# Softmax sums on VectorE, a 16-row tile inside v's projection, weight splits in quarters: one change to a hybrid decoder block

## The chip, the cores and the metric

The kernel runs on one core of one Trainium2 chip. The metric is the device time of one execution in microseconds (us). TensorE is written PE, its weight loads PEld, VectorE DVE, ScalarE ACT, GpSimd POOL, SyncE SP.

## The reference

One decoder block on 1,024 tokens of width 1,024, all in float32, with 16 meta tokens put in front (1,040 rows):

```python
h = rmsnorm(x, norm_g)
proj = jnp.einsum('bld,dn->bln', h, w_in)
u_pool, z_pool, q, k, v, z_attn, f_logit, g_pool, g_attn = jnp.split(proj, _split_points(), axis=-1)
y_pool = causal_multiscale_pool(u_pool, pool_w, pool_scale) * jax.nn.silu(z_pool)
log_f = jax.nn.log_sigmoid((f_logit + b_forget).astype(jnp.float32))
y_attn = forgetting_attention(q, k, v, log_f).reshape(B, L, ATTN_WIDTH) * jax.nn.silu(z_attn)
merged = (jax.nn.sigmoid(g_pool) * jnp.einsum('blc,cd->bld', y_pool, w_up_pool)
          + jax.nn.sigmoid(g_attn) * jnp.einsum('blc,cd->bld', y_attn, w_up_attn))
return x + jnp.einsum('bld,de->ble', merged, w_out)
```

The attention has 8 heads of width 64. Its logits get the running sum of `log_f`, a causal mask and a softmax over the keys. A last rmsnorm follows.

## The kernel before

Every float32 product is made of three products of float32r operands: each operand is split into a high part (a copy rounded to float32r) and a low part (the operand less its high part), and PE adds high x high, high x low and low x high (`g_mm3`, L131, the matmul in L139). So each weight matrix costs one copy on ACT (L127, tile `whi`) and one subtraction on POOL (L128, tile `wlo`, 128x1024 elements in one operation).

**Prologue.** Nine tiles of x (eight of 128 rows, the last of 16) are loaded, normalised (`norm_stat`, `norm_scale`) and turned by PE against an identity matrix (`norm_t`, L187, into the PSUM tiles `pt` and `pn`). ACT copies the result as `hh` (L189), DVE subtracts for `hl` (L190). Between these tiles stand the projections of q, k and v for the first pair of heads, in four column pieces each (the list `todo`; n counts them). In this part the order on all engines is the one in which the code stands (`manual_schedule`). `norm_t` of the last tile, with 16 rows, comes after piece n = 8 (v, columns 512 to 767), and piece n = 9 (q, columns 768 to 1039) needs its `hh`. Behind the last piece the weights of the forget gate are loaded (`wf`) and split by DVE (`wfs`, L443 and L444), and PE multiplies with them (L456, function `gates`).

**Attention.** From here on only PE's order is the code's; a scheduler sets the order on DVE, ACT, POOL and SP. There are 16 units: 4 pairs of heads x 2 heads x 2 halves of 512 queries, with 5 or 9 blocks of 128 keys. The steps of unit i + 1 that make logits (`qk`: PE L540 and L541 into `ps`, ACT L549 or DVE L547 into `S`, the maximum over blocks `m` on DVE, L556) are interleaved with the steps of unit i that make the softmax (`soft`: DVE L580 subtracts the maximum, ACT L581 takes the exponential, ACT L584 and DVE L585 split it into `ph` and `pl`, POOL L593 adds it up over the blocks in `acc`, PE L601 multiplies with v into `po`). Between the steps PE is given matmuls of projections that are not yet needed (`Fill`, `F.pull`), whose weights come through L127 and L128. They take most of PE's time.

At the end of a unit `maxes` (L561 to L571) takes the maximum over the 128 keys of `m`: DVE transposes 32x32 blocks into `mt`, reduces them (`mr`), combines the four groups of partitions with small copies and maxima (`mx`, `ms`, `my`, `mz`) and transposes back into the PSUM tile `pt`, from which the next unit's `soft` subtracts. `finish` evacuates `po` and sums `acc` over its 128 partitions:

```python
nc.scalar.copy(up_[:nu], acc[64:])
nc.vector.tensor_tensor(acc[:nu], acc[:nu], up_[:nu], op=ALU.add)
nc.scalar.activation(fold[:64], acc[:64], AF.Copy)
nc.vector.tensor_tensor(fold[64:], acc[:64], r32(fold)[:64], op=ALU.subtract)
```

(L614 to L617; the tiles are named `pl` and `ph` after the buffers that they share). One matmul with ones (`total`, L621, into `pt`) then sums the partitions, and ACT (L623, `ls`) and a DMA bring one row of 512 sums to DRAM (`sums`).

**End.** After the last unit come the rest of the projections, the pooling mixer (DVE L757, POOL L722), the reciprocal of the sums (L830, `lall`, stored as `recs`), the gates, the up projections (`up`, with `up_weights`) and the output projection (L892) with the final norm. `recs` is read back as `rc`, broadcast over 64 partitions (L739).

Of the kernel before, what the change touches and what calls it, by code (L numbers as in the profile page):

```python
# [8 lines left out]
F32 = mybir.dt.float32  # L9
# [10 lines left out]
H = 8  # L20
# [17 lines left out]
NPH = 3  # L38
LAG = 2
NRC = 2  # L40
REC0 = 2
EVAC = (((0, 1),), ((0,), (1,)))
WARM = (4, 1)

# [1 line left out]
def r32(ap):  # L46
    return ap.bitcast(F32)
# [7 lines left out]
def tile_hybrid_block(ctx, tc, x, meta, norm_g, w_in, b_forget, pool_w, pool_scale,  # L55
# [60 lines left out]
    hh = [hh4[k // 4][:, k % 4, :] for k in range(KO)]  # L116
    hl = [hl4[k // 4][:, k % 4, :] for k in range(KO)]

    def split_w(srcs, pool=None, tags=("wh", "wl"), eng=None):
# [7 lines left out]
        nc.scalar.activation(hi, raw, AF.Copy)  # L127
        (eng or nc.gpsimd).tensor_tensor(lo, raw, r32(hi), op=ALU.subtract)  # L128
        return hi, lo

    def w_chunk(col, **kw):  # L131
# [16 lines left out]
    def run(g):  # L148
        for _ in g:
            pass  # L150
# [28 lines left out]
    def norm_t(i0, xt, n):  # L179
        c0 = i0 * 128  # L180
        for j in range(2):
            if (2 * i0 + j) % 3 == 2:
                pt = psG.tile([128, 4, 128], F32, name="pn")
            else:
                pt = psT.tile([128, 4, 128], F32, name="pt")
            for i in range(4):
                nc.tensor.transpose(pt[:, i, :n], xt[:n, (4 * j + i) * 128:(4 * j + i + 1) * 128], ident[:n, :n])  # L187
            h_ = hh4[j][:, :, c0:c0 + n]
            nc.scalar.activation(h_, pt[:, :, :n], AF.Copy)  # L189
            last = nc.vector.tensor_tensor(hl4[j][:, :, c0:c0 + n], pt[:, :, :n], r32(h_), op=ALU.subtract)  # L190
        return last
# [200 lines left out]
    def ntok(i):  # L392
        return min(128, L - 128 * i)
# [41 lines left out]
    G_.close()  # L435
# [4 lines left out]
    wf = sm.tile([128, KO, H], F32, name="wf", bufs=1)  # L440
    nc.sync.dma_start(wf, w_in2[:, :, COL_F:COL_F + H])
    wfs = sm.tile([128, KO, 2 * H], F32R, name="wfs", bufs=1)
    nc.vector.tensor_copy(wfs[:, :, :H], wf)  # L443
    nc.vector.tensor_tensor(wfs[:, :, H:], wf, r32(wfs[:, :, :H]), op=ALU.subtract)  # L444
    SM.close()

    def gates():
# [15 lines left out]
        z, lf, u, d, one, car = [sm.tile([KB, NB, H], F32, name=n, bufs=1) for n in ("fz", "lf", "fu", "fd", "fo", "car")]  # L463
# [33 lines left out]
    pwl = sm.tile([128, 4, 128], F32R, name="pwl", bufs=1)  # L497

    exps, dves = [], []
    sums = dr.tile([H, SEQ], F32, name="sums")  # L500
    recs = dr.tile([H, SEQ], F32, name="recs")
    for p in range(4):
        spill["y", p] = dr.tile([128, SEQ], F32, name=f"sp_y{p}")

    class Unit:
# [98 lines left out]
        def finish(self):  # L604
            hr, lr = rows(self.e)
            po, acc = self.po, self.acc
            t = ap_.tile([128, 512], F32, name="t")
            nc.scalar.activation(t[hr], po[lr], AF.Copy)
            nc.vector.tensor_tensor(t[hr], po[hr], t[hr], op=ALU.add)
            nc.sync.dma_start(spill["y", self.p][hr, self.q0:self.q0 + 512], t[hr])  # L610
            fold = ap_.tile([128, 512], F32R, name="ph", bufs=NPH)
            up_ = r32(ap_.tile([128, 512], F32R, name="pl", bufs=NPH))
            nu = KB - 64
            nc.scalar.copy(up_[:nu], acc[64:])  # L614
            nc.vector.tensor_tensor(acc[:nu], acc[:nu], up_[:nu], op=ALU.add)  # L615
            nc.scalar.activation(fold[:64], acc[:64], AF.Copy)
            nc.vector.tensor_tensor(fold[64:], acc[:64], r32(fold)[:64], op=ALU.subtract)  # L617

            def total():
                pr = psT.tile([128, 512], F32, name="pt")  # L620
                nc.tensor.matmul(pr, onesr, fold, start=True, stop=True)  # L621
# [5 lines left out]
            return [total]  # L627

    def merged(a, c, extra=()):
        extra = list(extra)  # L630
# [7 lines left out]
        for i, (_, (w, dve, pe, f)) in enumerate(sorted(out_, key=lambda t: t[0])):  # L638
            f()
            if i >= REC0 and extra:  # L640
                extra.pop(0)()
            F.pull(max(0.0, PACE * dve - pe))

    cols = {"gp": COL_GP, "ga": COL_GA, "za": COL_ZA, "zp": COL_Z}
# [21 lines left out]
    late = []  # L666
    for i, u in enumerate(units):
        nxt = units[i + 1] if i + 1 < 16 else None
        F.now = i
        if nxt is not None and nxt.p != u.p:  # L670
            F.until(f"q{nxt.p}", f"k{nxt.p}")
        merged(list(nxt.a_steps()) if nxt else [], list(u.c_steps()), late)
# [8 lines left out]
        late = u.finish()  # L681
        if nxt is not None and nxt.p != u.p:
            F.until(f"v{nxt.p}")
            pair_fill(nxt.p + 1)
    for f in late:
        f()
    F.drain()
    last_dve = dves[-1]
    A.close()
# [45 lines left out]
    def attn_out(p):  # L735
        rc = btile("rc")
        for e in range(2):
            h = 2 * p + e
            after(nc.sync.dma_start(rc[rows(e)[0]], recs[h:h + 1, :].to_broadcast([64, SEQ])), stores[-1])  # L739
# [85 lines left out]
    split2 = pool_split(2)  # L825
    silu(zp[3])
    silu(zp[2])
    lall = sm.tile([128, 64], F32, name="lall", bufs=1)
    nc.sync.dma_start(lall, sums.rearrange("h (a b) -> (h a) b", b=64))
    after(nc.vector.reciprocal(lall, lall), split2)  # L830
# [127 lines left out]
```

## Time and profile before

| | |
|---|---|
| median of 3 runs | 767.85 us (767.46, 769.21, 767.85) |
| the profiled execution | 769.11 us, of which the span from the first to the last instruction is 767.4 us |
| mean granted PE clock in it | 0.997 of full speed |
| busy share of the span | PE 98%, PEld 83%, DVE 65%, ACT 51%, POOL 36% |

A line of a timeline gives start and duration in us, the engine, the line of the code, the operation, `out<-in`, the shapes and the number of instructions merged; in square brackets stands the idle time of the engine before it and who ended it. A line of the groups gives the busy time in us and the mean of one in ns, then the idle time before them. A line of the chain gives start, duration, engine, tile, line and count. PE's matmuls are pipelined, so the duration of one is longer than the step from one start to the next; how fast PE works is read from the steps.

### The profile page before, as it was taken

To read this page: it belongs to the slowest core of one execution; us is meant where nothing else is said; L and a number is where in the kernel's file an instruction comes from. 1 tells how busy PE (TensorE), PEld (TensorE's weight loads), DVE (VectorE), ACT (ScalarE), POOL (GpSimd) and SP (SyncE) were. 2 spreads that over 40 slices of the span, in tenths; PEclk is the share of its full clock that TensorE was granted. 3 is DMA by queue.
4 is the path that set the end of the run, shared out by engine and by line. 5 is a ranking of instruction groups with operands and counts; after the bars stand their busy time and mean duration, and the time that the engine had idled before them with its cause. 6 is when DMAs were issued, how large, how long until landed. Compare 5 with 4: busy or idle time off the path is not lost.

```text
span 767.4 us, 10526 instructions
## 1 busy us (share of the span) xinstructions
PE 751.6 (98%) x3762; PEld 638.5 (83%) x3762; DVE 497.1 (65%) x933; ACT 394.6 (51%) x756; POOL 278.1 (36%) x227
## 2 busy tenths in 40 slices
PE   8999999999999999999999999999999999999996
PEld 6996989988888898888988888888888688888885
DVE  5653578659779888598688866882465566434232
ACT  6652556456566655665655556551744554323112
POOL 4321235346326435433354263342374122322111
PEclk9999999999999999999999999999999999999999
DMA  9301122231221222221223232339357654523331
GB/s 304 73 18 39 28 82 74 67 97 49 62 58 52 72 75 70 77 63 41 77 62 103 71 103 62 103 108 373 123 176 177 233 176 128 191 83 113 107 110 55
DMA packets 73782, 79.33 MB, mean 103 GB/s; under 512 B 5473, under 2 KB 56673, under 8 KB 73730
## 3 DMA queue, kind: packets, MB, share of 16 engines
q1 hardware_dynamic: 68976, 63.46, 27.0%
q10 hardware_dynamic: 4754, 15.21, 6.0%
q8 instruction: 29, 0.48, 0.3%
q14 instruction: 23, 0.19, 0.1%
HBM read 57.58 MB, written 21.07 MB: 102 GB/s over the span
## 4 chain that ended last, share of the span: by engine, by line
PE 79%; DVE 8%; ACT 2%; issue 2%; DMA 2%; POOL 1%; POOLq 0%; DVEq 0%; SPq 0%; ACTq 0%
PE pj L139 57%; PE pj L892 12%; PE po L601 4%; PE ps L541 2%; PE ps L540 2%; DVE pl L585 1%; DVE S L580 1%; DMA rl<-sp_gp 1%; PE pj L456 1%; DVE ka L243 1%; POOL yl L722 1%; ACT S L549 1%; DMA rc<-recs 1%; DVE m L556 1%; DVE acc L615 0%
## 5 line engine op out<-in xcount | busy, mean ns | idle before, releaser
L139 PE MATMUL pj<-hh,whi 128*128 128x512 f32 (+4 forms) x768 | 179.9, 362 | 1.7 <-ACT hh L189 1.1
L139 PE MATMUL pj<-hl,whi 128*128 128x512 f32 (+4 forms) x768 | 178.0, 361 | 0.0
L139 PE MATMUL pj<-hh,wlo 128*128 128x512 f32 (+4 forms) x768 | 175.7, 360 | 0.0
L128 POOL TENSOR_TENSOR wlo<-raw,whi 128x1024 fp32r<-128x1024 f32 x37 | 91.7, 2478 | 223.7 <-ACT whi L127 90.5
L139 PEld LDWEIGHTS pj<-hh,whi 128*128 128x128 f32 x768 | 132.8, 190 | 19.6 <-ACT hh L189 1.2
L139 PEld LDWEIGHTS pj<-hh,wlo 128*128 128x128 f32 x768 | 133.2, 190 | 18.2
L139 PEld LDWEIGHTS pj<-hl,whi 128*128 128x128 f32 x768 | 132.5, 190 | 17.7
L585 DVE TENSOR_TENSOR pl<-S,ph 128x512 fp32r<-128x512 f32 (+4 forms) x112 | 87.1, 793 | 19.9 <-ACT ph L584 18.9
L593 POOL TENSOR_TENSOR acc<-acc,S 128x272 f32<-128x272 f32 (+4 forms) x80 | 77.5, 969 | 12.6 <-ACT S L581 6.6
L549 ACT ACTIVATE S<-ps,negc 128x400 f32<-128x400 f32 (+2 forms) x96 | 49.1, 515 | 46.7 <-DVE S L547 40.4
L581 ACT ACTIVATE S<-S 128x512 f32<-128x512 f32 (+4 forms) x112 | 49.4, 477 | 29.0 <-DVE S L580 28.9
L556 DVE TENSOR_TENSOR m<-m,S 128x272 f32<-128x272 f32 (+4 forms) x80 | 46.7, 583 | 22.3 <-ACT S L549 21.0
L584 ACT ACTIVATE ph<-S 128x512 fp32r<-128x512 f32 (+4 forms) x112 | 52.4, 478 | 11.6 <-PE po L601 10.8
L580 DVE TENSOR_TENSOR S<-S,pt 128x512 f32<-128x512 f32 (+4 forms) x112 | 51.7, 498 | 0.8
L892 PE MATMUL pj<-woh,gl 128*128 128x512 f32 (+1 forms) x136 | 51.8, 381 | 0.0
L892 PE MATMUL pj<-wol,gh 128*128 128x512 f32 (+1 forms) x136 | 51.6, 379 | 0.0
L892 PE MATMUL pj<-woh,gh 128*128 128x512 f32 (+1 forms) x136 | 51.6, 379 | 0.0
L816 POOL TENSOR_TENSOR gl<-rl,gh 128x512 fp32r<-128x512 f32 x16 | 23.2, 1454 | 72.3 <-ACT gh L815 72.3
L294 ACT ACTIVATE st<-pj 128x512 f32<-128x512 f32 x48 | 28.4, 592 | 39.7 <-PE pj L139 21.5
L127 ACT ACTIVATE whi<-raw 128x1024 fp32r<-128x1024 f32 x37 | 39.0, 1054 | 17.2 <-PE pj L139 10.6
L812 DVE TENSOR_TENSOR rl<-pj,rl 128x512 f32<-128x512 f32 x32 | 22.0, 689 | 31.8 <-PE pj L139 28.4
L540 PE MATMUL ps<-qa,ka 128*128 128x512 f32 (+4 forms) x112 | 36.4, 325 | 2.2 <-ACT S L549 2.1
(168 smaller groups left out, 1136.4 us busy)
## 6 DMA issues: line engine op xcount, KB each, us to landing
raw<-in_w_in_dram SPq DMA_DIRECT2D x40, 512.0 KB, 4.0
sp_gp<-st SPq DMA_DIRECT2D x16, 256.0 KB, 2.0
sp_ga<-st SPq DMA_DIRECT2D x16, 256.0 KB, 4.5
rl<-sp_gp ACTq DMA_DIRECT2D x8, 512.0 KB, 3.8
rl<-sp_ga ACTq DMA_DIRECT2D x8, 512.0 KB, 4.6
rawo<-in_w_out_dram SPq DMA_DIRECT2D x8, 512.0 KB, 3.1
xr<-in_x_dram SPq DMA_DIRECT2D x8, 512.0 KB, 4.3
xt<-in_x_dram SPq DMA_DIRECT2D x7, 512.0 KB, 8.3
```

Of the source, the lines that this page charges most:

```text
L127: nc.scalar.activation(hi, raw, AF.Copy)
L128: (eng or nc.gpsimd).tensor_tensor(lo, raw, r32(hi), op=ALU.subtract)
L139: nc.tensor.matmul(ps, a, b, start=(i == 0), stop=(i == len(seq) - 1))
L540: nc.tensor.matmul(ps[:kb, c0:], ka[:, k0:k0 + kb], qa[:, q0 + c0:q0 + 512], start=True, stop=False)
L549: nc.scalar.activation(s[:kb, f0:], ps[:kb, f0:], AF.Identity, bias=nb_)
L556: nc.vector.tensor_tensor(m[:kb, c0:], m[:kb, c0:], s[:kb, c0:], op=ALU.max)
L580: nc.vector.tensor_tensor(s[:kb, c0:], s[:kb, c0:], self.pm[:kb, c0:], op=ALU.subtract)
L581: exps.append(nc.scalar.activation(s[:kb, c0:], s[:kb, c0:], AF.Exp))
L584: nc.scalar.activation(ph[:kb, c0:], s[:kb, c0:], AF.Copy)
L585: dves.append(nc.vector.tensor_tensor(pl[:kb, c0:], s[:kb, c0:], r32(ph[:kb, c0:]), op=ALU.subtract))
L593: nc.gpsimd.tensor_tensor(acc[:kb, c0:], acc[:kb, c0:], s[:kb, c0:], op=ALU.add)
L892: nc.tensor.matmul(ps[:, :c1 - c0], mg[k][a][:, r], wo[k][b][:, c0:c1], start=(k == 0 and n == 0), stop=(k == KO - 1 and n == 2))
```

## The change

1. **Sums.** `finish` no longer folds `acc` and PE no longer sums it. DVE transposes `acc` in 32x32 blocks into a tile of the name `mt` and reduces it to 128x16 (`sr`); a DMA stores these partial sums, 64 bytes for each partition. `total`, `late`, the argument `extra` of `merged` and the constant `REC0` go. Before the reciprocal, four DMAs (one for each pair of heads) load the partial sums as 128x256 (`fin`), DVE adds the groups of four, takes the reciprocal and transposes 128x64 back.
2. **16-row tile.** `norm_t` of the last tile is called in the middle of piece n = 8, behind 16 of its 24 matmuls, in place of behind it.
3. **Gate weights.** The load of `wf` stands in piece n = 4, the split `wfs` in piece n = 8.
4. **Weight splits.** L128 becomes four operations of 128x256. The splits of the first three matrices (L383) stay whole.
5. Five small tiles of `gates` become slices of one tile `fz`, whose place `fin` takes later.

The words that came with the change also name four pool up projections ahead. The code of `up`, of `up_weights` and of the loop that calls them is the same in both files, and on PE no matmul behind the last unit stands in another place.

```diff
         nc.scalar.activation(hi, raw, AF.Copy)
-        (eng or nc.gpsimd).tensor_tensor(lo, raw, r32(hi), op=ALU.subtract)
+        for k in range(0, KO, 2):
+            nc.gpsimd.tensor_tensor(lo[:, k:k + 2], raw[:, k:k + 2], r32(hi[:, k:k + 2]), op=ALU.subtract)
...
-            run(v_piece(0, wv, t0, t1))
-        i = {0: 2, 1: 3, 3: 4, 4: 5, 6: 6, 7: 7, 8: 8}.get(n)
+            g = v_piece(0, wv, t0, t1)
+            if n == 8:
+                for _ in range(2 * KO):
+                    next(g)
+                norm_t(8, xts[8], ntok(8))
+            run(g)
+        i = {0: 2, 1: 3, 3: 4, 4: 5, 6: 6, 7: 7}.get(n)
...
+        if n == 4:
+            wf = sm.tile([128, KO, H], F32, name="wf", bufs=1)
+            nc.sync.dma_start(wf, w_in2[:, :, COL_F:COL_F + H])
+        if n == 8:
+            wfs = sm.tile([128, KO, 2 * H], F32R, name="wfs", bufs=1)
+            nc.vector.tensor_copy(wfs[:, :, :H], wf)
+            nc.vector.tensor_tensor(wfs[:, :, H:], wf, r32(wfs[:, :, :H]), op=ALU.subtract)
...
-            nc.scalar.copy(up_[:nu], acc[64:])
-            nc.vector.tensor_tensor(acc[:nu], acc[:nu], up_[:nu], op=ALU.add)
-            nc.scalar.activation(fold[:64], acc[:64], AF.Copy)
-            nc.vector.tensor_tensor(fold[64:], acc[:64], r32(fold)[:64], op=ALU.subtract)
...
-                nc.tensor.matmul(pr, onesr, fold, start=True, stop=True)
-                ls = ap_.tile([1, 512], F32, name="ls")
-                nc.scalar.copy(ls, pr[:1])
-                h = 2 * self.p + self.e
-                nc.sync.dma_start(sums[h:h + 1, self.q0:self.q0 + 512], ls)
+            at = ap_.tile([KB, 512], F32, name="mt")
+            after(nc.vector.transpose(at, acc), dves[-1])
+            r = sm.tile([128, 16], F32, name="sr")
+            nc.vector.tensor_reduce(r, at.rearrange("p (j b) -> p j b", b=32), axis=AX.X, op=ALU.add)
+            nc.sync.dma_start(sums[4 * self.p + 2 * self.e + self.half], r)
...
-    nc.sync.dma_start(lall, sums.rearrange("h (a b) -> (h a) b", b=64))
-    after(nc.vector.reciprocal(lall, lall), split2)
-    nc.sync.dma_start(recs.rearrange("h (a b) -> (h a) b", b=64), lall)
+    for p in range(4):
+        nc.sync.dma_start(lall[32 * p:32 * p + 32],
+                          sums[4 * p:4 * p + 4].rearrange("u (a r) j -> r u a j", r=32))
+    after(nc.vector.tensor_reduce(rall.rearrange("p (u j) -> p u j", u=4), lall.rearrange("p u a j -> p u j a"),
+                                  axis=AX.X, op=ALU.add), split2)
+    nc.vector.reciprocal(rall, rall)
+    nc.vector.transpose(fin[:, 320:], rall)
+    nc.sync.dma_start(recs.rearrange("(b p) r -> p b r", p=128), rect)
```

What this does to the order of instructions is shown at three places. The first is PE in the prologue, at the end of piece n = 8 (the rows of `pj` with 256 columns) and the start of piece n = 9 (272 columns); a row `x4` is four matmuls, and `-` and `+` are before and the change:

```order
+L187 MATMUL pt<-ident,xt 128x16 x4
+L187 MATMUL pn<-ident,xt 128x16 x4
 L139 MATMUL pj<-hh_112,wlo 128x256 x4
 L139 MATMUL pj<-hh_113,wlo 128x256 x4
-L187 MATMUL pt<-ident,xt 128x16 x4
-L187 MATMUL pn<-ident,xt 128x16 x4
 L139 MATMUL pj<-hh_112,whi 128x272 x4
 L139 MATMUL pj<-hh_113,whi 128x272 x4
```

The eight transposes of the 16-row tile move ahead of the last eight matmuls of the v piece, so that these stand between the transposes and the q piece that needs `hh`.

The second is DVE at the end of the prologue. Before:

```order
L190 TENSOR_TENSOR hl_114<-pt,hh_112 128x4x16
L190 TENSOR_TENSOR hl_115<-pn,hh_113 128x4x16
L222 SCALAR_TENSOR_TENSOR ql<-pj,qa 64x272 x2
L243 TENSOR_TENSOR ka<-pj,ka 64x272 x2
L262 TENSOR_TENSOR V<-pj,V 128x2x64 x2
L443 CAST wfs<-wf 128x8x8
L444 TENSOR_TENSOR wfs<-wf,wfs 128x8x8
```

The same place with the change:

```order
L190 TENSOR_TENSOR hl_114<-pt,hh_112 128x4x16
L190 TENSOR_TENSOR hl_115<-pn,hh_113 128x4x16
L443 CAST wfs<-wf 128x8x8
L444 TENSOR_TENSOR wfs<-wf,wfs 128x8x8
L222 SCALAR_TENSOR_TENSOR ql<-pj,qa 64x272 x2
L243 TENSOR_TENSOR ka<-pj,ka 64x272 x2
L262 TENSOR_TENSOR V<-pj,V 128x2x64 x2
```

The two operations on the gate weights pass the six operations that belong to the last q, k and v pieces.

The third is DVE between the first unit and the second, where the maximum of the next unit is finished. Before:

```order
L556 TENSOR_TENSOR m<-m,S 128x16
L615 TENSOR_TENSOR acc<-acc,pl 64x512
L561 STREAM_TRANSPOSE mt<-m 128x512
L563 TENSOR_REDUCE mr<-mt 128x16
L617 TENSOR_TENSOR ph<-acc,ph 64x512
L565 COPY mx<-mr 64x16 x2
L566 TENSOR_TENSOR ms<-mr,mx 128x16
L568 COPY my<-ms 32x16 x4
L569 TENSOR_TENSOR mz<-ms,my 128x16
L571 STREAM_TRANSPOSE pt<-mz 128x512
```

The same place with the change:

```order
L565 TENSOR_TENSOR m<-m,S 128x16
L570 STREAM_TRANSPOSE mt<-m 128x512
L572 TENSOR_REDUCE mr<-mt 128x16
L574 COPY mx<-mr 64x16 x2
L621 STREAM_TRANSPOSE mt<-acc 128x512
L575 TENSOR_TENSOR ms<-mr,mx 128x16
L623 TENSOR_REDUCE sr<-mt 128x16
L577 COPY my<-ms 32x16 x4
L578 TENSOR_TENSOR mz<-ms,my 128x16
L580 STREAM_TRANSPOSE pt<-mz 128x512
```

Two operations on `acc` stood ahead of `pt` before, two other ones stand there now, and both now come behind `mx`; the scheduler does the same at nearly all unit ends. On PE the one thing that changes behind the prologue is that the 16 matmuls with ones are gone.

More of the change, by code (lines that the diff above doesn't have):

```diff
@@ L40 @@
 NRC = 2
-REC0 = 2
 EVAC = (((0, 1),), ((0,), (1,)))
@@ L439, in tile_hybrid_block @@
     nc.sync.dma_start(psc, pool_scale[0].rearrange("(g c) -> c g", c=128))
[L440 to L444, printed above, removed]
     SM.close()
@@ L462, in gates @@
             nc.tensor.transpose(pt[:, b * 16:(b + 1) * 16], fT[:, KS[b]:KS[b] + KB], ident[:16, :16])
-        z, lf, u, d, one, car = [sm.tile([KB, NB, H], F32, name=n, bufs=1) for n in ("fz", "lf", "fu", "fd", "fo", "car")]
+        fz = sm.tile([KB, 384], F32, name="fz", bufs=1)
+        z, lf, u, d, one = [fz[:, n * NB * H:(n + 1) * NB * H].rearrange("p (b h) -> p b h", h=H) for n in range(5)]
+        car = sm.tile([KB, NB, H], F32, name="car", bufs=1)
         pv = pt[:, :NB * 16].rearrange("p (b j h) -> p b j h", j=2, h=H)
@@ L499, in tile_hybrid_block @@
     exps, dves = [], []
-    sums = dr.tile([H, SEQ], F32, name="sums")
-    recs = dr.tile([H, SEQ], F32, name="recs")
+    sums = dr.tile([16, 128, 16], F32, name="sums")
+    recs = dr.tile([256, 32], F32, name="recs")
     for p in range(4):
@@ L610, in finish, with merged @@
             nc.sync.dma_start(spill["y", self.p][hr, self.q0:self.q0 + 512], t[hr])
[L611 to L615, printed above, removed]
-            nc.scalar.activation(fold[:64], acc[:64], AF.Copy)
[L617 to L621, printed above, removed]
-                ls = ap_.tile([1, 512], F32, name="ls")
-                nc.scalar.copy(ls, pr[:1])
-                h = 2 * self.p + self.e
-                nc.sync.dma_start(sums[h:h + 1, self.q0:self.q0 + 512], ls)
-            return [total]
-    def merged(a, c, extra=()):
-        extra = list(extra)
+            at = ap_.tile([KB, 512], F32, name="mt")
[3 more added lines that the diff above has]
+            nc.sync.dma_start(sums[4 * self.p + 2 * self.e + self.half], r)
+    def merged(a, c):
         out_ = []
@@ L637, in merged @@
                 acc += s[0]
-        for i, (_, (w, dve, pe, f)) in enumerate(sorted(out_, key=lambda t: t[0])):
+        for _, (w, dve, pe, f) in sorted(out_, key=lambda t: t[0]):
             f()
-            if i >= REC0 and extra:
-                extra.pop(0)()
             F.pull(max(0.0, PACE * dve - pe))
@@ L665, in tile_hybrid_block @@
     units[0].maxes(FIRST)
-    late = []
     for i, u in enumerate(units):
@@ L671, in tile_hybrid_block @@
             F.until(f"q{nxt.p}", f"k{nxt.p}")
-        merged(list(nxt.a_steps()) if nxt else [], list(u.c_steps()), late)
+        merged(list(nxt.a_steps()) if nxt else [], list(u.c_steps()))
         for b in range(u.nb - LAG, u.nb):
@@ L680, in tile_hybrid_block @@
             nxt.maxes()
-        late = u.finish()
+        u.finish()
         if nxt is not None and nxt.p != u.p:
@@ L684, in tile_hybrid_block @@
             pair_fill(nxt.p + 1)
-    for f in late:
-        f()
     F.drain()
@@ L737, in attn_out @@
         for e in range(2):
-            h = 2 * p + e
-            after(nc.sync.dma_start(rc[rows(e)[0]], recs[h:h + 1, :].to_broadcast([64, SEQ])), stores[-1])
+            rw = recs.rearrange("(h c) r -> h (c r)", h=H)[4 * e + p:4 * e + p + 1]
+            after(nc.sync.dma_start(rc[rows(e)[0]], rw.to_broadcast([64, SEQ])), stores[-1])
         nc.vector.tensor_tensor(Y[p], Y[p], rc, op=ALU.mult)
@@ L827, in tile_hybrid_block @@
     silu(zp[2])
-    lall = sm.tile([128, 64], F32, name="lall", bufs=1)
-    nc.sync.dma_start(lall, sums.rearrange("h (a b) -> (h a) b", b=64))
-    after(nc.vector.reciprocal(lall, lall), split2)
-    nc.sync.dma_start(recs.rearrange("h (a b) -> (h a) b", b=64), lall)
+    fin = sm.tile([128, 384], F32, name="fin", tag="fz", bufs=1)
+    lall = fin[:, :256].rearrange("p (u a j) -> p u a j", u=4, a=4)
+    rall = fin[:, 256:320]
+    rect = fin[:, 320:].rearrange("p (b r) -> p b r", b=2)
+    for p in range(4):
[6 more added lines that the diff above has]
+    nc.sync.dma_start(recs.rearrange("(b p) r -> p b r", p=128), rect)
     pool_chain(1)
```

2 lines of the change are left out of this document (1 added, 1 removed).

## The prediction

> **What bounds the kernel now.** I read first the busy times, then the chain of work that ended last, then the stretches by stage, then PE's waits.
>
> ```profile
> PE 751.6 (98%) x3762; PEld 638.5 (83%) x3762; DVE 497.1 (65%) x933; ACT 394.6 (51%) x756; POOL 278.1 (36%) x227
> PE 79%; DVE 8%; ACT 2%; issue 2%; DMA 2%; POOL 1%; POOLq 0%; DVEq 0%; SPq 0%; ACTq 0%
> 513.88 58.58 PE pj L139 x253
> 88.00:514.00 426.00, 422.84 (x2157) 367.66 (x2156) 334.20 (x682) 254.57 (x525) 180.60 (x139) 1.00 0.25 72
> 572.00:604.00 32.00, 30.17 (x126) 23.28 (x126) 21.16 (x24) 15.21 (x20) 10.24 (x6) 1.00 0.63 184
> PE ps L540 <- ACT S L549: 2.1, 3, 1.1
> ```
>
> PE is busy nearly always, and the chain is PE's. The third row, of the chain, is a stretch in which PE waits for nothing: 58.58 / 253 = 0.232 us is the step of one matmul with 512 columns. The stretches (behind the two bounds their length, then PE's busy time) show PE idle for 3.16 us in the attention and for 1.83 us ahead of the attention's up projections. The last row is the largest of PE's waits in the attention (us in total, times, longest). So time can come only from work that leaves PE or from PE's few waits, and whatever the change frees on DVE, ACT or POOL counts only where PE stands behind it.
>
> **The matmuls with ones.** What leaves PE:
>
> ```profile
> L621 PE MATMUL pt<-ph,onesr 128*128 128x512 f32 x16 | 6.4, 401 | 0.0
> ```
>
> By the step, not by the pipelined 401 ns: 16 x 0.232 = **3.7 us**. They stand amid matmuls that wait for nothing, so PE simply gets to the next ones sooner.
>
> **The 16-row tile.** DVE, PE and ACT at that place:
>
> ```profile
> 43.23 1.39 DVE L176 SCALAR_TENSOR_TENSOR xt<-xt,rstd,gb 16x512 f32<-16x512 f32 x2 [0.65 <-POOL rstd L111]
> 45.52 0.69 DVE L190 TENSOR_TENSOR hl<-pn,hh 128x512 fp32r<-128x512 f32 x1
> 43.65 1.10 PE L139 MATMUL pj<-hl,whi 128*128 128x256 f32 x8
> 44.59 1.10 PE L139 MATMUL pj<-hh,wlo 128*128 128x256 f32 x8
> 46.27 0.42 PE L187 MATMUL pn<-ident,xt 16*128 16x16 f32 x4 [0.24 <-DVE hl L190]
> 47.05 0.28 ACT L261 ACTIVATE V<-pj 128x128 fp32r<-128x128 f32 x1 [3.37 <-DVE V L262]
> 47.48 0.23 ACT L189 ACTIVATE hh<-pt 128x64 fp32r<-128x64 f32 x1
> 47.77 1.27 PE L139 MATMUL pj<-hh,whi 128*128 128x272 f32 x8 [1.08 <-ACT hh L189]
> ```
>
> The transposes now come up at 44.6, where DVE has just finished `xt` (43.23 + 1.39). But those into `pn` need the bank that DVE reads until 46.21, as before, so they still start at 46.27, now with v's last eight matmuls queued behind them. Those take 0.94 (43.65 to 44.59) and end near 47.5. ACT, held until 47.05 by v's blocks, then takes `hh` ahead of v's evacuation: from 47.33 at the latest, 0.23 long. PE and `hh` are both there at about 47.5, in place of 47.77: **0.3 us**. Bounds: 0, if ACT frees no earlier, and 1.3 (0.24 + 1.08), if DVE gets to `hl` sooner. Most of the stall only moves to the other side of eight matmuls.
>
> **A slow PE behind that stall.**
>
> ```profile
> 48.88 1.77 PE L139 MATMUL pj<-hl,whi 128*128 128x272 f32 x8
> 50.45 2.01 PE L139 MATMUL pj<-hh,wlo 128*128 128x272 f32 x8
> 52.26 1.31 PE L139 MATMUL pj<-hh,whi 128*128 128x272 f32 x8
> 53.41 1.16 PE L139 MATMUL pj<-hl,whi 128*128 128x272 f32 x8
> 54.41 1.16 PE L139 MATMUL pj<-hh,wlo 128*128 128x272 f32 x8
> 49.17:52.57 3.40, 3.40 (x17) 3.40 (x17) 0.00 (x0) 1.13 (x2) 0.00 (x0) 0.50 0.02 5
> 103.78:107.19 3.41, 1.78 (x11) 1.30 (x9) 2.25 (x3) 3.41 (x10) 2.29 (x4) 1.00 0.00 0
> ```
>
> Eight such matmuls take 1.00 us from start to start (53.41 to 54.41). Those from 48.88 took 1.57, from 50.45 1.81, from 52.26 1.15: together 1.5 us too long. The stretch in the sixth row shows why: a granted clock of 0.50 (third number from the end) for 3.4 us, right behind the stall. If the idle time drew it, a prologue in which PE works again from 46.3 on may not: **1.5 us**, or 0. Against it speaks the last row, a stretch with PE busy for 1.78 of 3.41 us and behind it no slow clock in the attention. I take 1.5, as this is the one slow stretch and the one stall among short matmuls. The Trainium skill (TensorE: Matmul & The Clock Gate, Part 1) has the gate halve the clock after at least one idle window of about 3.4 us, with windows that run free of the kernel. The longest wait here was 1.1 us, so the trace does not agree with the first; by the page the stall did not draw the slow clock, and this term would be 0.
>
> **The gate weights.**
>
> ```profile
> 57.63 1.17 PE L139 MATMUL pj<-hh,wlo 128*128 128x272 f32 x8
> 58.33 0.92 DVE L443 CAST wfs<-wf 128x64 fp32r<-128x64 f32 x1
> 59.66 1.54 PE L456 MATMUL pj<-hh,wfs 128*16 128x384 f32 x8 [0.86 <-DVE wfs L444]
> ```
>
> PE is through with v at 57.63 + 1.00 = 58.63 and starts on the gates at 59.66. The cast waits for no one but DVE's own queue. With the change both operations follow the 16-row tile, near 48, and DVE has nothing to do in the stretch from 49.17 (0.00 above). So this wait goes whole: **1.0 us**. It comes back, by at most as much, if PE then meets a bank that DVE has not yet emptied; no row shows that.
>
> **Unit ends.** DVE loses two operations of a unit and gains two; the new ones have the shapes of the third and the fourth row:
>
> ```profile
> L615 DVE TENSOR_TENSOR acc<-acc,pl 64x512 f32<-64x512 f32 x16 | 12.4, 778 | 0.5 <-ACT pl L614 0.2
> L617 DVE TENSOR_TENSOR ph<-acc,ph 64x512 fp32r<-64x512 f32 x16 | 11.8, 738 | 0.3
> L561 DVE STREAM_TRANSPOSE mt<-m 128x512 f32<-128x512 f32 x16 | 11.3, 706 | 0.3
> L563 DVE TENSOR_REDUCE mr<-mt 128x16 f32<-128x512 f32 x16 | 10.8, 675 | 0.2
> 241.99 1.04 ACT L127 ACTIVATE whi<-raw 128x1024 fp32r<-128x1024 f32 x1
> 252.23 0.85 PE L139 MATMUL pj<-hh,whi 128*128 128x512 f32 x3
> ```
>
> 1.38 us stand in place of 1.52, both times ahead of `pt`, so `pt` comes 0.1 us sooner. ACT loses three operations a unit; PE waits for none of them. On SP the loads of sums now wait for stores, with stores and weight loads queued behind: the closest weights that I found are the last two rows, ready 9.2 us ahead of PE, and only a longer hold-up would reach PE.
>
> POOL's quarters are covered by the same lead. Their effect lies elsewhere:
>
> ```profile
> L128 POOL TENSOR_TENSOR wlo<-raw,whi 128x1024 fp32r<-128x1024 f32 x37 | 91.7, 2478 | 223.7 <-ACT whi L127 90.5 <-PE pj L139 39.4 <-ACT S L549 23.9
> L593 POOL TENSOR_TENSOR acc<-acc,S 128x272 f32<-128x272 f32 x16 | 15.8, 986 | 3.6 <-ACT S L581 2.3 <-PE ps L541 0.7
> 93.47 2.61 DVE L556 TENSOR_TENSOR m<-m,S 128x144 f32<-128x144 f32 x2 [0.20 <-ACT S L549]
> 93.62 2.44 POOL L128 TENSOR_TENSOR wlo<-raw,whi 128x1024 fp32r<-128x1024 f32 x1 [11.62 <-ACT S L549]
> 252.97 2.50 DVE L615 TENSOR_TENSOR acc<-acc,pl 64x512 f32<-64x512 f32 x1 [0.18 <-ACT pl L614]
> 245.87 3.85 POOL L593 TENSOR_TENSOR acc<-acc,S 128x400 f32<-128x400 f32 x4
> 256.10 0.35 DVE L565 COPY mx<-mr 64x16 f32<-64x16 f32 x2
> ```
>
> A quarter is nearest to the second row, so at most 1.0 us, and four cost at most 1.5 us more than the whole. The third and the fourth row end together: two small maxima on DVE, the second started inside POOL's operation, stand until POOL is done. Beside a quarter DVE comes free after at most 1.0 in place of 2.4, 1.4 us sooner, and on that chain hang the first waits for `ps`. Of their 2.1 us I take 1.2; of the other 1.1 us of PE's idle time in the attention 0.6, since the fold that was held up to 2.50 us (fifth row) is gone. Together **1.8 us**, between 3.2 (no wait left) and -1.5: the scheduler also reorders subtractions and splits, and as many new waits of 1.1 us and less may come.
>
> **The end.**
>
> ```profile
> 544.53 0.54 DVE L830 RECIPROCAL lall<-lall 128x64 f32<-128x64 f32 x1
> 581.00 4.95 SPq L739 DMA_DIRECT2D rc<-recs  x8
> ```
>
> The added reduction of 128x256 and transpose of 128x64 are smaller than the 0.68 and 0.71 above and have 36 us until `recs` is read back: nothing. The up projections, which the change names, stand where they stood: nothing.
>
> **Sum.** 3.7 + 0.3 + 1.5 + 1.0 + 1.8 = 8.3, from the profiled 769.11 (the 1.7 us outside its span stay): 760.8. That execution is 1.26 above the median of 767.85. If the median run had no slow clock, the sum without that term, 6.8, gives 761.0; the two meet.
>
> **Rivals.** (a) *The slow clock does not hang on the stall*, or the new gap draws it too: 769.11 - 6.8 = 762.3. For it speaks the busy share of 1.78 that drew none. (b) *Only what is counted goes*: nothing at the tile, the clock and the unit ends: 769.11 - 4.7 = 764.4. For it speaks that PE's order is fixed and that other queues are reordered without regard to its waits. (c) *All waits of the attention and the tile go*: 769.11 - 3.7 - 1.0 - 1.3 - 1.5 - 3.2 = 758.4, and from the median 757.1. (d) *Slower: DVE waits for POOL's `acc`.* The new transpose waits for it with `ms` to `pt` and the next unit's subtractions queued behind. If each quarter is held by a DVE operation of 0.8, a matrix takes 4 x 1.8 = 7.2 in place of 2.5, 4.7 more. At the unit end of the last three rows `acc` is done at 249.7, and the transpose would come up where `mx` ends, less the vanished 2.50: 253.9. So it decides from 4.2 us of delay; two matrices ahead of `acc` would make 9.4, 5.2 too late. At the eight ends of units with nine blocks that is 42 us, and if PE's filling hides half, 760.8 + 21 = 782. Against it: POOL idles 224 us ahead of these splits, so a delay is caught up before the next unit.
>
> **Chances.** Forecast 0.52; (a) 0.18; (b) 0.13; (c) 0.10; (d) 0.05; within 0.2% of before 0.02 (0.2%, 1.5 us, is about what a measurement of this kernel can tell from no change). Faster: 0.52 + 0.18 + 0.13 + 0.10 = 0.93. The range goes from (c), 757.1, to (b), 764.4, and leaves out (d) and what lies between.
>
> **What would show it.** Right: 16 matmuls fewer on PE; no wait for `wfs`; the q piece at about 47.5 and no clock of 0.50 behind it; two-input operations on DVE held for 1.0 at most beside a quarter; fewer waits for `ps`, PE idle in the attention below 2 us. Wrong: DVE waiting for POOL ahead of the transpose of `acc`; PE idle there for more than 4 us; PE waiting for `whi` or `wlo`; a tail in which `rc` comes later against PE than now.

## The result and the profile after

The changed kernel takes 759.82 us (median of 4 runs, 758.1 to 760.59), the kernel before on the same chip 768.53 (4 runs): a ratio of 0.9888, 95% interval 0.9871 to 0.9905. The two profiled executions took 758.10 and 769.11, 11.0 apart where the medians are 8.7 apart. In the 58 runs beside the experiments the kernel before has medians of 767.51 to 767.72, and from these the changed kernel is 7.7 to 7.9 us away.

The busy times, the groups and the stretches of the changed kernel (in a row of the stretches the first number behind the bounds and the length is PE's busy time, and the third from the end is the granted clock):

```profile
PE 744.6 (98%) x3746; PEld 633.6 (84%) x3746; DVE 489.0 (65%) x935; ACT 370.4 (49%) x708; POOL 307.8 (41%) x338
PE 90%; DVE 3%; issue 1%; ACT 0%; POOLq 0%; POOL 0%; DVEq 0%; ACTq 0%
L128 POOL TENSOR_TENSOR wlo<-raw,whi 128x256 fp32r<-128x256 f32 x148 | 121.8, 853 | 199.2 <-ACT whi L126 103.9
49.00:52.50 3.50, 3.50 (x30) 3.50 (x29) 0.00 (x0) 2.35 (x5) 1.25 (x2) 1.00 0.02 5
88.00:514.00 426.00, 425.27 (x2166) 370.17 (x2165) 332.18 (x682) 230.22 (x476) 208.76 (x233) 1.00 0.27 78
PE ps L549 <- ACT S L558: 0.5, 1, 0.5
```

PE has 16 matmuls fewer. The chain is now 90% PE's, from 79%. PE is idle for 0.73 us in the attention, from 3.16, and its waits for `ps` fell from 2.1 to 0.5. No clock of 0.50 stands where it stood before.

The places of the prologue in the changed kernel:

```profile
46.46 0.42 PE L187 MATMUL pn<-ident,xt 16*128 16x16 f32 x4 [1.18 <-DVE hl L190]
47.85 1.17 PE L139 MATMUL pj<-hh,whi 128*128 128x272 f32 x8
48.01 0.18 DVE L443 CAST wfs<-wf 128x64 fp32r<-128x64 f32 x1
56.12 1.17 PE L139 MATMUL pj<-hh,wlo 128*128 128x272 f32 x8
57.12 1.21 PE L463 MATMUL pj<-hh,wfs 128*16 128x384 f32 x6
```

The q piece starts at 47.85, not at 47.5: from the eight matmuls of v ahead of the tile (43.83, then 43.65) it is 4.02 in place of 4.12, so 0.1 us. PE now waits 1.18 us ahead of v's last eight matmuls: the stall moved, as foreseen. The gates follow without a gap (56.12 + 1.00).

The two small maxima that stood with POOL for 2.61 us before, on DVE:

```profile
90.93 0.94 DVE L565 TENSOR_TENSOR m<-m,S 128x144 f32<-128x144 f32 x2 [0.20 <-ACT S L558]
```

They take 0.94, beside a quarter. Start by start against the profiled execution before, PE's matmuls are 2.5 us earlier at the gates, 10.1 at the end of the attention (7.5 in it) and 11.1 at the attention's up projections. The last 1.0 was not forecast: PE's wait of 1.1 for `whu` is absent. In the profiles of the experiments that wait comes and goes: 0.7 to 0.9 in the three with the old sums, none in five with the new ones and 0.5 to 1.8 in four. ACT's sigmoid ahead of `whu` waits there for the load of `sp_gp`. What makes that load late stays open.

### The profile page after: what moved, and what is told of

It reads as the page before. It is cut to its first block, busy times and chain, and to the rows that moved or that the text cites. A ratio compares the mean times of both kernels' runs of the same rounds, so it can differ in the third digit from the quotient of the medians.

```text
span 756.4 us, 10583 instructions
## 1 busy us (share of the span) xinstructions
PE 744.6 (98%) x3746; PEld 633.6 (84%) x3746; DVE 489.0 (65%) x935; ACT 370.4 (49%) x708; POOL 307.8 (41%) x338
## 4 chain that ended last, share of the span: by engine, by line
PE 90%; DVE 3%; issue 1%; ACT 0%; POOLq 0%; POOL 0%; DVEq 0%; ACTq 0%
PE pj L139 67%; PE pj L891 12%; PE po L610 5%; PE ps L550 3%; PE ps L549 2%; PE pj L463 1%; PE pj L256 0%; DVE rl L803 0%; DVE yal L735 0%; DVE S L589 0%; DVE y L731 0%; DVE m L565 0%; ACT S L558 0%; DVE ka L243 0%; DVE xt L176 0%
## 5 line engine op out<-in xcount | busy, mean ns | idle before, releaser
L128 POOL TENSOR_TENSOR wlo<-raw,whi 128x256 fp32r<-128x256 f32 x148 | 121.8, 853 | 199.2 <-ACT whi L126 103.9
L565 DVE TENSOR_TENSOR m<-m,S 128x272 f32<-128x272 f32 (+4 forms) x80 | 41.4, 518 | 23.9 <-ACT S L558 22.2
L556 DVE SCALAR_TENSOR_TENSOR S<-ps,negc,mask 128x128 f32<-128x128 f32 (+2 forms) x72 | 23.7, 330 | 23.0 <-PE ps L550 22.2
```

Of the source, the lines that this page charges most:

```text
L128: nc.gpsimd.tensor_tensor(lo[:, k:k + 2], raw[:, k:k + 2], r32(hi[:, k:k + 2]), op=ALU.subtract)
L565: nc.vector.tensor_tensor(m[:kb, c0:], m[:kb, c0:], s[:kb, c0:], op=ALU.max)
```

## The experiments

Every time is a median of 4 to 12 runs beside the kernel before on the same chip; the ratio is to that kernel, with its 95% interval. The last column gives the mean granted clock of the timed runs. One stretch of 3.4 us at half clock takes 0.002 from it. It sorts the runs only roughly, as every profile also ends with 1.3 to 4.0 us at half clock: that of the eighths stands at 0.997 and has no such stretch ahead of its end.

| kernel | us (range) | ratio | clock |
|---|---|---|---|
| changed kernel | 759.82 (758.1 to 760.59) | 0.9888 (0.9871 to 0.9905) | 0.995 to 0.999 |
| prologue alone | 766.42 (765.88 to 768.19) | 0.9989 (0.9980 to 0.9999) | 0.996 to 0.999 |
| new sums alone | 767.16 (764.85 to 767.76) | 0.9986 (0.9976 to 0.9995) | 0.993 to 0.998 |
| quarters alone | 764.85 (763.29 to 765.12) | 0.9954 (0.9942 to 0.9967) | 0.997 to 0.999 |
| changed, whole splits | 766.95 (764.24 to 768.17) | 0.9977 (0.9963 to 0.9991) | 0.993 to 0.997 |
| changed, halves | 763.84 (762.79 to 765.71) | 0.9948 (0.9933 to 0.9963) | 0.994 to 0.999 |
| changed, eighths | 758.25 (757.37 to 760.30) | 0.9879 (0.9864 to 0.9895) | 0.995 to 0.999 |
| changed, old sums | 763.05 (762.31 to 764.36) | 0.9931 (0.9912 to 0.9949) | 0.996 to 0.999 |
| changed, ones kept | 762.98 (761.50 to 764.31) | 0.9940 (0.9928 to 0.9953) | 0.995 to 0.999 |
| changed, late gate weights | 760.19 (758.31 to 761.79) | 0.9892 (0.9874 to 0.9911) | 0.996 to 0.999 |
| changed, late tile | 759.78 (758.25 to 760.91) | 0.9884 (0.9866 to 0.9901) | 0.995 to 0.998 |
| changed, one bank | 757.38 (756.98 to 757.87) | 0.9869 (0.9853 to 0.9884) | 0.997 to 0.998 |
| changed, one bank, eighths | 757.99 (757.84 to 758.27) | 0.9875 (0.9861 to 0.9888) | 0.998 |

**Whole splits in the changed kernel.**

```diff
-        for k in range(0, KO, 2):
-            nc.gpsimd.tensor_tensor(lo[:, k:k + 2], raw[:, k:k + 2], r32(hi[:, k:k + 2]), op=ALU.subtract)
+        if True:
+            nc.gpsimd.tensor_tensor(lo, raw, r32(hi), op=ALU.subtract)
```

> The changed kernel with GpSimd's weight split as one operation of 128x1024 again, nothing else changed; the order on every engine stays. Theory (the prediction's): VectorE's operations with two inputs are held beside a whole split, up to about 2.2 us each, and TensorE's waits for ps in the attention come back: the part of the run from 88 us to 514 us takes 1.8 us longer than in the changed kernel (between 1.2 and 3.2), POOL's mean of one operation goes from 0.85 to about 2.5 us, and the time is about 761.6. Rival 1: those waits went because the fold at the end of a unit is gone, not because of the quarters: at most 0.5 us more, 760.0. Rival 2: the quarters cost something elsewhere on the path: the time gets shorter, 759 or less.

Measured 766.95, 7.1 above the changed kernel, far beyond what any theory had given. Its waits, stretches and one place on POOL, DVE and PE:

```profile
PE po L610 <- DVE pl L594: 2.1, 2, 1.6
PE ps L549 <- ACT S L558: 1.9, 2, 1.1
88.00:514.00 426.00, 421.48 (x2136) 365.89 (x2136) 347.97 (x678) 227.41 (x474) 181.15 (x139) 1.00 0.26 74
349.37 2.38 POOL L128 TENSOR_TENSOR wlo<-raw,whi 128x1024 fp32r<-128x1024 f32 x1 [0.42 <-ACT whi L126]
349.74 2.31 DVE L565 TENSOR_TENSOR m<-m,S 128x272 f32<-128x272 f32 x1 [0.46 <-ACT S L558]
351.98 0.43 DVE L594 TENSOR_TENSOR pl<-S,ph 128x272 fp32r<-128x272 f32 x1
350.50 0.37 PE L610 MATMUL po<-ph,V 128*128 128x272 f32 x1
352.46 0.39 PE L610 MATMUL po<-pl,V 128*128 128x272 f32 x1 [1.59 <-DVE pl L594]
349.79:353.20 3.41, 1.82 (x11) 1.45 (x10) 3.05 (x3) 0.81 (x3) 1.96 (x1) 1.00 0.07 12
353.21:356.62 3.41, 3.41 (x11) 2.73 (x10) 2.87 (x9) 0.79 (x4) 0.00 (x0) 0.50 0.50 142
```

The chain can be read off: `m`, started 0.37 inside POOL's split, stands until the split is through; `pl` comes behind it on DVE, and PE waits for `pl`. The stretch in which PE waited is followed by 3.4 us at half clock: the wait is paid twice. Start by start PE loses 6.7 us in the attention against the changed kernel, 3.2 of them at this place; the order of the instructions on DVE, ACT and PE is the same in both. In the changed kernel the same `m`, begun 0.36 inside four quarters that run from 344.96, takes 0.67, and PE does not wait there:

```profile
345.32 0.67 DVE L565 TENSOR_TENSOR m<-m,S 128x272 f32<-128x272 f32 x1 [0.46 <-ACT S L558]
348.11 0.29 PE L610 MATMUL po<-pl,V 128*128 128x272 f32 x1
```

The Trainium skill (SBUF — State Buffer, Who interferes with whom) says that a VectorE instruction with two SBUF inputs and a GpSimd one that reads SBUF shut each other out for a whole instruction; these rows agree, 2.31 us against 0.67.

**Halves and eighths.** As above with `range(0, KO, 4)` and `range(KO)`.

> The changed kernel with GpSimd's weight split in two operations of 128x512. Theory B (a two-input operation of VectorE that starts beside a split stands until that one operation of GpSimd is done, and the wait's length is what TensorE pays): longest hold about 1.3 us, between whole and quarters, by proportion of the holds (2.45, 1.25, 0.85) a quarter of the 6.8 us: 761.5, between 760.5 and 763. Rival: it is the number of operations or their order that counts, and halves are as slow as the whole: 766 or more.

> The changed kernel with GpSimd's weight split in eight operations of 128x128. Theory B: the longest hold falls to about 0.5 us, but TensorE has only 0.7 us of waits left in the attention: 759.3 to 759.9. Rival: the fixed part of eight operations makes GpSimd late with acc, and VectorE's transpose of acc waits for it with the next unit's subtractions behind: 761 or more.

Measured 763.84, above the 763 of theory B and below its rival, and 758.25, below both theories. The halves' profile has a wait of 1.7 for `pl` at the same place and, in its stretches, the half clock behind it:

```profile
PE po L610 <- DVE pl L594: 1.7, 1, 1.7
352.12:355.53 3.41, 3.41 (x10) 2.75 (x9) 2.97 (x10) 0.27 (x1) 0.00 (x0) 0.50 0.47 135
```

Whole, halves, quarters and eighths make 766.95, 763.84, 759.82 and 758.25: the time follows the length of one operation of POOL, not the number or their sum (POOL's busy time grows from 181 to 232 us in the attention), with the same order on DVE, ACT and PE in all four. It does not follow the holds in proportion: of the 7.1 us between whole and quarters 4.0 are left at halves, where theory B had a quarter. Between quarters and eighths the ranges overlap.

**Quarters alone, and the new sums alone,** in the kernel before.

```diff
 (quarters alone)
-        (eng or nc.gpsimd).tensor_tensor(lo, raw, r32(hi), op=ALU.subtract)
+        for k in range(0, KO, 2):
+            nc.gpsimd.tensor_tensor(lo[:, k:k + 2], raw[:, k:k + 2], r32(hi[:, k:k + 2]), op=ALU.subtract)
 (the new sums alone: the kernel before with points 1 and 5 of the change)
-            return [total]
+            at = ap_.tile([KB, 512], F32, name="mt")
+            after(nc.vector.transpose(at, acc), dves[-1])
...
```

> The kernel before with GpSimd's weight split in quarters, nothing else. Theory A (the prediction's size): the holds of VectorE beside a split were worth 1.8 us to TensorE: 765.7. Theory B (after the run with whole splits): the quarters are the largest part of the change by themselves; the changed kernel with the old sums stands at 763.05, of which gate weights and tile explain at most 0.4: 763.2 to 764.0. Theory C: the quarters help only together with the new sums: 767 or more.

> The kernel before with the new way to the softmax sums, nothing else: whole splits, the 16-row tile and the gate weights where they stood. Theory A (the prediction's term): 16 matmuls of 0.232 us leave TensorE and nothing comes back: 763.9. Theory B: with whole splits the freed time is given back as TensorE waits behind VectorE's held operations (po for pl, ps for S): 766.5 to 767.5, and TensorE idle for more than 4 us between 88 us and 514 us.

Measured 764.85, between A and B, and 767.16, as B had it. The first row is from the stretches of the quarters alone; then come rows of the new sums alone and, last, of the kernel before:

```profile
88.00:514.00 426.00, 424.85 (x2168) 370.39 (x2167) 325.88 (x682) 256.56 (x526) 204.24 (x230) 1.00 0.26 75
```

```profile
88.00:514.00 426.00, 420.97 (x2144) 365.50 (x2143) 349.44 (x681) 227.97 (x477) 181.21 (x139) 1.00 0.26 73
351.09 2.31 DVE L558 TENSOR_TENSOR m<-m,S 128x272 f32<-128x272 f32 x1 [0.47 <-ACT S L551]
351.84 0.37 PE L603 MATMUL po<-ph,V 128*128 128x272 f32 x1
353.80 0.39 PE L603 MATMUL po<-pl,V 128*128 128x272 f32 x1 [1.59 <-DVE pl L587]
```

```profile
353.07 2.33 DVE L556 TENSOR_TENSOR m<-m,S 128x272 f32<-128x272 f32 x1 [0.47 <-ACT S L549]
355.14 0.37 PE L601 MATMUL po<-ph,V 128*128 128x272 f32 x1
355.81 0.40 PE L601 MATMUL po<-pl,V 128*128 128x272 f32 x1 [0.30 <-DVE pl L585]
```

This is where a part of the 16 matmuls' gain goes. Before and with the new sums alone the same `m` is held as long (2.33, 2.31). Before, PE comes to `po<-ph` 2.07 us behind the start of `m` and waits 0.30; with less to do it comes 0.75 behind it and waits 1.59. PE is idle for 5.0 us in the attention. The rest goes with the slow clock: 10 of the 12 timed runs have a mean clock of 0.993 to 0.996 and a median of 767.22; the two at 0.997 and 0.998 took 764.85 and 764.96. The profile is of the run at 0.998 and has no half clock ahead of its end, so that the waits draw it in the other runs is concluded from their clocks and not seen.

What each kernel gains in the attention without any half clock is read between two starts of PE, the first in the gates and the first behind the last `po`. The second start is shown for the kernel before (its gates start at 59.66) and for the changed kernel (57.12), then both for the quarters alone and for the new sums alone:

```profile
513.72 1.09 PE L139 MATMUL pj<-hh,whi 128*128 128x512 f32 x4
503.65 1.40 PE L139 MATMUL pj<-hh,whi 128*128 128x512 f32 x5
57.81 0.86 PE L457 MATMUL pj<-hh,wfs 128*16 128x384 f32 x4 [0.28 <-DVE wfs L445]
508.19 1.09 PE L140 MATMUL pj<-hh,whi 128*128 128x512 f32 x4
58.17 1.03 PE L456 MATMUL pj<-hh,wfs 128*16 128x384 f32 x5 [0.84 <-DVE wfs L444]
510.52 1.40 PE L139 MATMUL pj<-hh,whi 128*128 128x512 f32 x5
```

From the one to the other it takes 454.06 us before, 446.53 in the changed kernel, 450.38 with the quarters alone and 452.35 with the new sums alone: 7.5, 3.7 and 1.7 less. So beside whole splits 2.0 of the 3.7 us of the matmuls come back as waits. The two gains alone make 5.4, 2.1 short of the changed kernel's 7.5.

**The old sums, and the matmuls with ones alone, in the changed kernel.** The first is the changed kernel without points 1 and 5 of the change; the second adds:

```diff
             nc.sync.dma_start(sums[4 * self.p + 2 * self.e + self.half], r)
+            pr = psT.tile([128, 512], F32, name="pt")
+            nc.tensor.matmul(pr, onesr, hh[0][:, :512], start=True, stop=True)
```

> The changed kernel with the kernel before's way to the softmax sums: the fold on VectorE and ScalarE, the 16 matmuls with ones, the reload as one row for a head. Quarters, the 16-row tile and the gate weights stay as changed. Theory: 16 matmuls of 0.232 us come back, 3.7 us, and up to 0.6 us of waits for the fold: 763.5 to 764.1. Rival 1: the transpose and the reduction on VectorE save nothing beyond the matmuls, and their waits cost: below 3.7, 762 to 763.4. Rival 2: more than counted went with the sums (ScalarE's three operations of a unit, the matmuls' weight loads): over 4.5 us, 764.4 or more.

> The changed kernel with 16 matmuls with ones put back on TensorE, one at each end of a unit, with hh as their data and nobody reading the result; the sums stay on VectorE. Theory (the prediction's term): 16 x 0.232 = 3.7 us, since TensorE waits for next to nothing: 763.5. Rival: the matmul at a unit's end falls into TensorE's own short waits and costs less: 761 to 762.5.

Measured 763.05 and 762.98: 3.2 each, below the 3.7 of the term; the first is in rival 1's range, the second between the theory and its rival. Start by start, from the gates to the end of the attention, the old sums cost PE 3.8 us and the bare matmuls 3.4, a step of about 0.2 at each unit end. So beside quarters the term holds to 0.5 us, and the fold's operations on ACT and DVE are worth 0.5 us at most.

**The gate weights late, the tile late, and both early alone.** In the changed kernel, each put back; then the kernel before with points 2 and 3 of the change.

```diff
 (late gate weights; the load of wf moves back too)
-        if n == 8:
-            wfs = sm.tile([128, KO, 2 * H], F32R, name="wfs", bufs=1)
...
 (late tile)
-                norm_t(8, xts[8], ntok(8))
...
-        i = {0: 2, 1: 3, 3: 4, 4: 5, 6: 6, 7: 7}.get(n)
+        i = {0: 2, 1: 3, 3: 4, 4: 5, 6: 6, 7: 7, 8: 8}.get(n)
```

> The changed kernel with the load of wf and the two operations that make wfs where they stood before, behind v's projection. Theory: TensorE waits 1.0 us for wfs ahead of the gates' first matmul and nothing later takes that up: 760.8, and the matmuls of the attention all start 1.0 us later than in the changed kernel, counted from the q piece. Rival: the cast is short now (0.18 us, where it stood beside a memset of GpSimd's before and took 0.92), so that the wait is 0.3 us or less: 760.0 to 760.1.

> The changed kernel with the 16-row tile's normalisation behind the whole of v's projection again. Theory: the stall of 0.24 + 1.08 us comes back ahead of the q piece, the tile itself costs 0.1 to 0.3 us, and the granted clock falls to 0.50 for 3.4 us right behind that stall, 1.5 us: 761.4 to 761.6 in the profiled execution. Rival 1: the slow clock comes by chance and not from the stall: no clock of 0.50 behind it, 760.0. Rival 2: the waits at the tile were moved and not removed, and moving them cost something: 759.8 or less.

> The kernel before with the 16-row tile within v's projection and the gate weights made early, nothing else: whole splits, old sums. Theory A (the prediction's terms): gate weights 1.0, tile 0.3, slow clock 1.5 where the profiled execution had it: 766.2 against a median with no slow clock of 767.5. Theory B (after the other runs): the tile is worth 0.1 and its stall only moves; the wait for wfs, 0.9 in the kernel before, goes whole; the slow clock still comes in part of the runs: 766.4 to 766.9, with clocks between 0.994 and 0.999. Rival: the freed time is given back at the held operations of the attention, as with the new sums alone: 767.2 or more.

Measured 760.19, 759.78 and 766.42. The late gate weights, in the timeline and the stretches:

```profile
57.66 1.17 PE L139 MATMUL pj<-hh,wlo 128*128 128x272 f32 x8
58.37 0.33 DVE L448 CAST wfs<-wf 128x64 fp32r<-128x64 f32 x1
59.10 1.21 PE L461 MATMUL pj<-hh,wfs 128*16 128x384 f32 x6 [0.28 <-DVE wfs L449]
43.59:47.00 3.41, 2.23 (x21) 1.98 (x20) 3.35 (x7) 0.30 (x2) 0.00 (x0) 1.00 0.00 0
47.00:50.41 3.41, 3.41 (x17) 3.41 (x18) 0.78 (x5) 0.89 (x4) 0.00 (x0) 0.50 0.00 0
```

With quarters the wait for `wfs` is only 0.44 (57.66 + 1.00 to 59.10), since the cast takes 0.33 there and not 0.92: the two parts of the change share this wait. And the half clock is there although the tile is early. In the late tile's profile it stands behind its own stall, too:

```profile
47.43 1.27 PE L139 MATMUL pj<-hh,whi 128*128 128x272 f32 x8 [1.08 <-ACT hh L189]
48.61:52.02 3.41, 3.41 (x17) 3.41 (x16) 0.00 (x0) 1.06 (x1) 0.00 (x0) 0.50 0.02 5
```

The move of the tile is worth next to nothing: one stall stands in place of another, and both draw the slow clock in part of the runs. The prologue's gain alone stays whole: its profile has PE busy for 422.84 us of the attention's 426, as before, and PE is as far ahead of the kernel before behind the attention (2.6 us, 1.5 of them the slow clock) as at the gates.

**One bank for the 16-row tile,** with v's block transposes moved behind it, then the same with eighths.

```diff
+        if n < 128:
+            pb = psT.tile([128, 8, 64], F32, name="pt")
+            for i in range(8):
+                nc.tensor.transpose(pb[:, i, :n], xt[:n, i * 128:(i + 1) * 128], ident[:n, :n])
...
-        if n in (4, 7, 10):
+        if n in (4, 8, 10):
             run(v_blocks(0, 2 * (n // 3) - 2, 2 * (n // 3)))
```

> The changed kernel with the eight transposes of the 16-row tile in one bank of psT (none into pn) and v's four block transposes behind that tile instead of ahead of it. Theory: the wait of 1.2 us for pn goes, hh of the tile is made while v's last eight matmuls run, and the q piece starts about 1.0 us sooner against v's first matmul; with that stall the slow clock at this place goes too: 1.0 to 2.0 us less than the changed kernel, 757.8 to 758.8, and granted clocks of 0.998 and more in most runs. Rival 1: the wait only moves on to hh or to the vt blocks: 759.5 or more. Rival 2: the slow clock comes wherever it likes: the time falls by 1.0 at most and the clocks of the runs scatter as before, between 0.995 and 0.999.

> The changed kernel with the 16-row tile in one bank, as in the run of that alone, and GpSimd's split in eighths. Theory: both edits take different waits, so they add up: 1.6 us from the eighths and 1.0 to 2.0 from the tile below the changed kernel, 756.2 to 757.2. Rival: the eighths' gain was the scatter of the slow clock: no more than the tile's, 757.8 or more.

Measured 757.38, below the forecast of 757.8 to 758.8, and 757.99, in the rival's range. With one bank, in the timeline and the stretches:

```profile
43.96 0.66 PE L184 MATMUL pt<-ident,xt 16*128 16x16 f32 x8
44.56 1.22 PE L139 MATMUL pj<-hh,wlo 128*128 128x256 f32 x8
45.75 0.75 PE L139 MATMUL pj<-hh,whi 128*128 128x272 f32 x4
46.78 0.77 PE L139 MATMUL pj<-hh,whi 128*128 128x272 f32 x4 [0.29 <-ACT hh L195]
44.00:50.00 6.00, 5.71 (x48) 5.47 (x48) 3.44 (x11) 2.52 (x8) 0.22 (x1) 1.00 0.01 3
```

The wait for `pn` is gone, and PE is idle for 0.29 of 6 us. The four runs lie within 0.9 us, at clocks of 0.997 and 0.998, where the changed kernel's spread over 2.5 at 0.995 to 0.999: by these few runs, what the edit takes away is a stall of 1.2 us and a slow clock that comes in some runs. This version has the lowest median. Eighths add nothing to it; their profile has a wait of 0.8 for `whu`, which that of one bank lacks.

## Why the prediction was right, and where it was not

The time came out 1.0 below the forecast of 760.8, in part by luck: two terms were wrong and nearly cancel, the unit ends 2 us too small and the slow clock 1.5 too large. For runs with a mean clock of 0.998 or more, 45 of the 58 of the kernel before, the median is 767.44; for the changed kernel's two it is 758.78: 8.7 us to explain. For the prologue alone it is 766.06, 1.4 less than before, of which 0.3 is a shorter wait for `whu`.

| term | predicted | measured | by |
|---|---|---|---|
| matmuls with ones | 3.7 | 3.2 to 3.8 beside quarters; without them 1.7 in the attention, 0.4 between medians | old sums, ones kept, new sums alone |
| 16-row tile | 0.3 | 0.1 | starts on PE, late tile |
| slow clock behind the stall | 1.5 | 0 between medians, 1.5 to 1.8 in runs that have it | clocks of 58 runs, quarters alone, prologue alone, late weights, one bank |
| gate weights | 1.0 | 1.0 beside whole splits, 0.4 beside quarters | prologue alone, late gate weights |
| unit ends | 1.8 | 3.7 to 4.1 | 7.5 in the attention less 3.4 to 3.8; quarters alone 3.7 |
| the end | 0 | 0, and a wait of up to 1.8 whose cause is open, 1.0 less in the changed kernel's profile | waits for `whu` |

- **Unit ends.** The mechanism was the right one, the size was not. "Of their 2.1 us I take 1.2; of the other 1.1 us of PE's idle time in the attention 0.6": nearly all of it went. The 3.2 taken as the most that could go was no bound either. A wait is listed from the end of a matmul whose duration reaches past the next start. In the whole-split run PE starts `po<-ph` at 350.50 and `po<-pl` at 352.46; eight steps of 272 columns take 1.00, so the delay is 1.96 - 0.12 = 1.84, listed as 1.59. Over some five waits of the attention (three of them for `ps`) that makes about 1 us more. The fold's 0.6 of the 1.8 was near its 0.5 at most; it is the quarters, put at 1.2, that give 3.7 alone, with the fold kept.
- **The slow clock.** "I take 1.5, as this is the one slow stretch and the one stall among short matmuls": with its clock of 0.997 the profiled execution belongs with the 13 in 58 below 0.998 (median 768.89), and two of the changed kernel's four runs are at 0.995 and 0.996 (760.18 and 760.59). Half of rival (a) was right, "or the new gap draws it too": the late gate weights' profile shows it. Its other half, that the clock does not hang on the stall, is not borne out: every slow stretch ahead of a profile's end stood right behind one in which PE was busy for 1.6 to 2.2 of 3.4 us, though not every such one drew it. The size was right where it comes: with the quarters alone the runs at 0.997 are 1.5 longer than those at 0.999. The Trainium skill (TensorE: Matmul & The Clock Gate, Part 1) asks for a whole idle window; none of the windows ahead of these stretches was idle, so the measurement decides against it. Its free-running window would fit a stall that draws the slow clock in some runs only.
- **The matmuls with ones.** "They stand amid matmuls that wait for nothing, so PE simply gets to the next ones sooner" is true of the changed kernel and false without the quarters: with the new sums alone PE gets sooner to DVE's held operations and loses 2.0 of the 3.7 us there. The terms were added as if they were independent; in the attention the sums alone give 1.7, the quarters 3.7 and the prologue nothing, together 5.4, and all at once 7.5. The medians, 0.4, 2.7 and 1.3 against 8.7, lie further apart, as these kernels differ in how many of their runs have the slow clock, and the 8.7 is taken from a median of 768.53.
- **The gate weights** were rightly costed from before. That the quarters take half of the same wait, with the cast at 0.33, was missed.
- **The 16-row tile.** That the stall only moves was right; its 0.3 came out as 0.1.
- **Rival (c)** came true in the attention, where PE is idle for 0.73 us, and not at the tile, where the stall stayed.
- **Rival (d)** did not come: in the attention DVE's waits name POOL once in the changed kernel, `DVE S L556 <- POOL wlo L128`, for 0.6 us. POOL's mean quarter of 0.853 lay within the bound of 1.0.
- **The end** and the up projections cost nothing, as said; the 1.0 gained at `whu` was not forecast.

## What to carry to other kernels

Here time taken from the busiest engine alone moved it against the engine behind it, and half of it came back as waits where that engine was held; time taken ahead of both stayed. So before work is taken off the bound, look for the longest operation that holds the next engine in line, and cut that operation: here its length, not its sum, set the loss. And of a clock or a wait seen in a single profile, ask first in how many runs it stands, and compare parts of a change by runs of the same clock.

## What the runs showed of the hardware that was not expected

- Slow stretches of 3.413 us at a granted clock of 0.50 follow waits far shorter than themselves: 1.18 us in the late gate weights' profile, 1.59 in that with whole splits. They begin a whole number of 3.413 us (9, 10, 99 and 170) behind the first clock record of their profile. Not every such wait draws one: in the changed kernel's profile the same wait of 1.18 drew none.
- A VectorE cast of 128x64 is held as well, though it has one input: 0.92 us in the kernel before, beside a memset of POOL, 0.33 to 0.35 beside the end of a quarter and 0.18 with POOL idle.
